# Output product and first up products of a decoder trunk: operands of y a block ahead, first combinations and up weights within the last block, a written order across the seam

## The chip, the cores and the metric

The kernel runs on one core of a Trainium2 chip. The metric is the device time of one execution in microseconds (us). The core has a matrix engine (TensorE, PE in the profile; the loading of its stationary operands is listed as PEld), a vector engine (VectorE, DVE), a scalar engine (ScalarE, ACT), a general engine (GpSimd, POOL) and SyncE (SP), which here issues all DMA transfers. Each engine works off its own queue in order; semaphores tie the queues together.

## The reference

A sequence of 2048 rows of width 1024, everything in float32. `mod` gives six vectors of the layer (shift, scale and gate of the mixer and of the FFN).

```python
h = rms_norm(x) * (1 + scale1) + shift1
p = h @ W_in                                  # all head groups in one projection
A, B, C = mlstm(p), forgetting_attention(p), gated_chunks(p)
x = x + gate1 * (concat(A, B, C) @ W_out)     # W_out 1024 x 1024
h = rms_norm(x) * (1 + scale2) + shift2
x = x + gate2 * ConvFFN(h)                    # up (d_ff 2816, twice), causal conv of width 3, SwiGLU, down
```

The change lies in the line with W_out, in the beginning of the up product, and in the last product of down.

## The kernel before, in words

The stages follow one another: projection, attention (until about 1124 us), the product with W_out, up, down. Each matrix operand is split into a rounded part (hi) and the remainder (lo), and `mm3` forms a product of two operands as three matmuls: hi by hi, hi by lo, lo by hi (lines L54, L55, L56). A split is a CAST on ACT (the hi) and a subtraction on DVE or POOL (the lo).

**The product with W_out.** The rows are done in four blocks of 512, in the order `TBS = (2, 3, 0, 1)`; so the second half of the sequence (H = 1) comes first. `Block.mm(i, nb)` makes 128 rows (i = 0..3) by 512 columns (nb = 0, 1) in one bank `wps`, from 8 k of y (`yhl`) and of W_out (`wo0` and `wo1`, its two halves of columns): 24 matmuls. One such (i, nb) is called a part. y is the mixer's output; it was stored to DRAM and is read back into the staging tiles `ld` (for the first four k from two places, which DVE adds), and then split. Before the change `Block.start` writes all 8 k at the head of the block that uses them, and the tiles come from two tags of 16 and 8 buffers.

`evict` multiplies a bank by the gate (`yg`), adds it to x and squares the result on ACT for the norm; `stats` turns the sums into a factor with a power on POOL (L128); `scale` multiplies the 1024 columns of x by it. When all four i of a block are scaled, `turns` transposes them: 8 k by 4 transposes of 128x128 into four banks `tps`, and for each k one ACTIVATE on ACT (L1240) that applies scale and shift and writes h (`hz`).

**Up.** The 22 groups of up weights for each half H are multiplied by a scheme with seven products p in place of eight, each on one combination of quarters of h: `OF = {1: "B11", 6: "T2", 2: "B21", 5: "T1", 7: "T3", 4: "T4", 3: "B22"}`. The B are quarters; T1, T3, T2 and T4 are differences. For the half that comes second (H = 1) the combinations are made during the output stage and stored (`put_d`, `hc_d`) and loaded again later; for the first half (H = 0) `b_first` makes them when it is needed: differences on DVE, CAST on ACT, lo on DVE (L1176 to L1185). A step is one product of one group: 12 matmuls into banks `ub`. The steps of the first two groups alternate: steps 0 and 1 use B11, 2 and 3 B21, 4 and 5 T1, 6 and 7 T2, 8 and 9 T3, 10 and 11 T4, 12 and 13 B22; step 14 is the first of the third group. `prep` makes the weights of a step three steps ahead: a sum or difference `S` of weight tiles `w` on DVE, then CAST (`wsph`, L1358) and lo (`wspl`, L1359) in 12 rotating buffers.

**Down** is made of seven products too, each of 11 steps k with four banks `db`; a step takes one k through all four banks. After the last step of the last product each bank goes through two operations on DVE (L1568, L1569) and out by DMA.

**What sets the order.** The program is written once in the order of the code; a scheduler then moves instructions within each engine's queue, and buffers (so many per tag) decide when a tile may be written again. Within `tc.manual_schedule()` it moves nothing, and each engine's queue follows the code. A pool is opened on the left or on the right side of the free memory and closed again, and a tile opened in a freed place waits for the last reader of what was there.

The matmuls of a step:

```python
def mm3(ps, lh, ll, rh, rl, start, stop, resume=False):
    T.matmul(ps, lh, rh, start=start, stop=False, skip_group_check=resume)
    T.matmul(ps, lh, rl, start=False, stop=False, skip_group_check=resume)
    T.matmul(ps, ll, rh, start=False, stop=stop, skip_group_check=resume)
```

## Time and profile before

| | |
|---|---|
| median of 3 runs | 2607.89 us (2607.47 to 2609.18) |
| the profiled execution | 2607.8 us, its span 2606.1 us |
| mean granted TensorE clock | 0.997 |
| output product, from the attention's last matmuls to its own last | 1124.57 to 1314.73 us |
| up, until its step 14 begins | 1314.73 to 1372.87 us |
| last matmul of down begins | 2599.58 us |

In a row of the timeline the columns are start (us), duration (us), engine, line, operation, output and inputs, shapes, count, and in square brackets the idle time of the engine before it with what ended it. A row "PE tps L1239 <- ACT hz L1240: 4.5, 3, 2.5" of the waits says that the matmuls of line 1239 into `tps` waited 4.5 us in total, three times, at most 2.5 us, for the operation of line 1240 on ACT.

### The profile page before, as it was taken

The page shows a single profiled execution, that of the slowest core. Times are in us where ns is not written, and L with a number is a line of the kernel's source. Part 1 is how long each engine was busy: PE and PEld are TensorE (multiplying, and loading weights), DVE is VectorE, ACT ScalarE, POOL GpSimd, SP SyncE. Part 2 cuts the span into 40 slices and gives each one's busy share as a digit, 9 for nine tenths or more (in the row PEclk, how much of TensorE's full clock was granted, in tenths as well). Part 3 has the DMA queues.
Part 4 walks back from the last instruction along what each step waited for, and adds up shares of the span by engine and source line. Part 5 has one row for each costly group of instructions (what it writes and reads, how often), then busy time and mean ns, then how long its engine had stood idle before and what let it go on. Part 6 is the DMA issues. An engine that isn't in the chain of part 4 may idle for free.

```text
span 2606.1 us, 36311 instructions
## 1 busy us (share of the span) xinstructions
PE 2530.5 (97%) x12521; PEld 2097.9 (81%) x12537; DVE 2010.0 (77%) x3438; ACT 1272.8 (49%) x2424; POOL 402.5 (15%) x532
## 2 busy tenths in 40 slices
PE   5999999999999999999989999999999999999999
PEld 5888888888787877777868888888888888888787
DVE  7657666476388889866589888888888887997797
ACT  4333343432388878844455544454444444444443
POOL 2012310132266556520000000000000000000000
PEclk9999999999999999999999999999999999999999
DMA  7345763454664445266632222255222217658523
GB/s 247 107 120 160 209 209 88 129 152 138 180 164 123 129 126 166 58 195 224 248 89 92 79 89 82 81 201 187 90 81 81 90 65 279 210 176 290 184 93 117
DMA packets 302592, 379.58 MB, mean 146 GB/s; under 512 B 31934, under 2 KB 194588, under 8 KB 300360
## 3 DMA queue, kind: packets, MB, share of 16 engines
q1 hardware_dynamic: 302408, 377.26, 46.1%
q8 instruction: 99, 1.62, 0.3%
q14 instruction: 85, 0.70, 0.1%
HBM read 276.44 MB, written 100.74 MB: 145 GB/s over the span
## 4 chain that ended last, share of the span: by engine, by line
PE 81%; DVE 9%; DMA 4%; ACT 3%; issue 2%; POOL 1%; SPq 0%; DVEq 0%; ACTq 0%; POOLq 0%
PE ub L56 11%; PE ub L54 11%; PE ub L55 11%; PE acc L54 6%; PE acc L56 6%; PE acc L55 6%; PE db L55 4%; PE db L56 4%; PE db L54 4%; PE sp L206 3%; PE tp L259 3%; PE op L245 2%; PE op L246 2%; PE wps L55 2%; PE wps L54 2%
## 5 line engine op out<-in xcount | busy, mean ns | idle before, releaser
L54 PE MATMUL acc<-wh,hh 128*128 128x512 f32 (+2 forms) x768 | 285.5, 373 | 1.9 <-DVE vhl L762 1.2
L54 PE MATMUL ub<-T,wsph 128*128 128x512 f32 x704 | 274.2, 390 | 5.8 <-ACT wsph L1358 5.8
L56 PE MATMUL ub<-T,wspl 128*128 128x512 f32 x704 | 273.7, 389 | 1.6 <-DVE wspl L1359 1.6
L56 PE MATMUL acc<-wh,hl 128*128 128x512 f32 (+2 forms) x768 | 274.2, 360 | 0.3 <-DVE hl L566 0.3
L55 PE MATMUL acc<-wl,hh 128*128 128x512 f32 (+2 forms) x768 | 273.9, 358 | 0.2
L55 PE MATMUL ub<-T,wsph 128*128 128x512 f32 x704 | 273.9, 389 | 0.0
L55 PE MATMUL db<-wspl,wsph 128*128 128x512 f32 x616 | 240.6, 391 | 3.6 <-DVE wspl L1490 3.5
L56 PE MATMUL db<-wsph,wspl 128*128 128x512 f32 x616 | 239.6, 389 | 0.0
L54 PE MATMUL db<-wsph 128*128 128x512 f32 x616 | 238.3, 389 | 0.3 <-ACT wsph L1489 0.3
L1358 ACT CAST wsph<-S 128x512 fp32r<-128x512 f32 x176 | 109.7, 623 | 228.4 <-PE ub L55 162.8
L263 DVE TENSOR_TENSOR plo<-tp,phi 128x512 fp32r<-128x512 f32 (+1 forms) x320 | 187.0, 607 | 31.6 <-ACT phi L262 29.4
L54 PE MATMUL ub<-B,wsph 128*128 128x512 f32 x528 | 207.1, 392 | 2.8 <-ACT wsph L1358 2.8
L56 PE MATMUL ub<-B,wspl 128*128 128x512 f32 x528 | 207.2, 392 | 0.6 <-DVE wspl L1359 0.6
L55 PE MATMUL ub<-B,wsph 128*128 128x512 f32 x528 | 207.0, 392 | 0.0
L223 ACT ACTIVATE L<-L,nm 128x1024 f32<-128x1024 f32 (+2 forms) x192 | 172.6, 903 | 36.0 <-DVE nm L212 34.7
L262 ACT CAST phi<-tp 128x512 fp32r<-128x512 f32 (+1 forms) x320 | 160.0, 521 | 40.2 <-PE tp L259 38.9
L259 PE MATMUL tp<-ident,L 128*128 128x128 f32 x1088 | 177.0, 274 | 2.5 <-POOL L L228 0.6
L206 PE MATMUL sp<-kk,q 128*128 128x512 f32 (+3 forms) x640 | 169.2, 375 | 3.3 <-DVE nm L212 2.2
L1489 ACT CAST wsph<-act 128x512 fp32r<-128x512 f32 x132 | 82.3, 623 | 179.0 <-PE db L55 162.2
L228 POOL TENSOR_SCALAR L<-L,rs 128x1024 f32<-128x1024 f32 (+2 forms) x192 | 167.2, 881 | 11.0
L56 PEld LDWEIGHTS acc<-wh,hl 128*128 128x128 f32 x768 | 145.0, 190 | 22.3 <-DVE hl L566 0.8
L54 PEld LDWEIGHTS acc<-wh,hh 128*128 128x128 f32 x768 | 146.2, 191 | 20.7 <-DVE vhl L762 1.4
(333 smaller groups left out, 5942.9 us busy)
## 6 DMA issues: line engine op xcount, KB each, us to landing
w<-in_w_up_dram SPq DMA_DIRECT2D x88, 512.0 KB
wd<-in_w_down_dram SPq DMA_DIRECT2D x176, 256.0 KB
wa<-in_w_ada_dram SPq DMA_DIRECT2D x96, 256.0 KB
act_d<-yc SPq DMA_DIRECT2D x44, 512.0 KB
act<-act_d SPq DMA_DIRECT2D x44, 512.0 KB
wr<-in_w_in_dram SPq DMA_DIRECT2D x64, 256.0 KB
q<-q_d SPq DMA_DIRECT2D x128, 128.0 KB
hc_d<-hl SPq DMA_DIRECT2D x28, 512.0 KB
```

Source lines behind the costliest of these rows:

```text
L54: T.matmul(ps, lh, rh, start=start, stop=False, skip_group_check=resume)
L55: T.matmul(ps, lh, rl, start=False, stop=False, skip_group_check=resume)
L56: T.matmul(ps, ll, rh, start=False, stop=stop, skip_group_check=resume)
L206: T.matmul(sp[:, b : b + bw], q2[n][:, qs], kk[:, s0 + b : s0 + b + bw], start=n == 0, stop=n == 1 and not last)
L223: A.activation(L[c], L[c], AF.Exp, bias=nm[:, n - 1 : n], scale=-1.0, accum_out=rs[:, c : c + 1])
L228: G.tensor_scalar(t, t, rs[:, 0:1], 1.0, op0=ALU.mult, op1=ALU.mult)
L245: T.matmul(op[:, c0:], vv[:, j, :], hi[:, c0:], start=(j == 0), stop=False)
L259: T.transpose(tp[:, i * P : (i + 1) * P], rows[i][j // 8][:, (j % 8) * P : (j % 8 + 1) * P], ident)
L262: A.copy(hi[:, c0:], tp[:, c0:])
L263: V.tensor_tensor(lo[:, c0:], tp[:, c0:], hi[:, c0:].bitcast(F32), op=ALU.subtract)
L1358: A.copy(hi, src)
L1489: A.copy(hi, v)
```

## The change

The parts of the change, in the order of the program:

- y is loaded and split one k at a time during the block before the one that uses it (`y_load`, `y_split`), into five staging tiles in place of three. Its tiles are the places `act4` to `act11` and `act14` to `act21`, which down uses later, one set for even blocks and one for odd.
- The second half of W_out is multiplied by the gate when it is loaded (`gain`), its lo are all made by DVE (before, every second one by POOL), and the eviction of the second half is one addition of bank and x.
- `turns` takes four k at a time: 16 transposes, a part of 24 matmuls, 16 transposes.
- The combinations that are stored for H = 1 are made a few operations at a time (`some`), and their four buffers are those of the up weights `w`.
- The last block runs by pairs of i (`by_two`). From its fifth part (n, j) = (3, 4) until step 14 of up the order is the written one. B11, B21 and the weights of the first up steps are made within the block's last parts, and the first step of up stands directly behind the block's last matmul.
- T1, T2, T3 and T4 and B22 of the first half lie in other tiles (`b_tile`), T1 and T3 are made with the next difference ahead of the present lo, and each is written at a fixed step.
- In down's last product the last three k are done bank by bank.
- The memset of `hal` goes from DVE to POOL, and pools that live across the seam (`keep_l`, `keep_r`) replace some that were closed there.

The core of the diff:

```diff
-        pool.open("wo_r", "right", ("yhl0", 2048, 16), ("ld", 2048, 3), ("wo0", 2048, 16))
-    def load_split(src, tag, eng, more=None):
+        pool.open("keep_r", "right", *[("act%d" % n, 4096, 1) for n in range(14, 22)])
+        pool.open("wo_r", "right", ("ld", 2048, 5), ("wo0", 2048, 16))
...
+        if gain is not None:
+            eng.tensor_tensor(t, t, gain, op=ALU.mult)
+        if pair:
+            both = pool.tile([P, 2, TB], F32R, name="yhl", tag=tag)
...
-    def load_w(nb):
+    def load_w(nb, gain=None):
         for k in range(KT):
             src = w_out[k * P : (k + 1) * P, nb * 512 : nb * 512 + 512]
-            wo.append(load_split(src, "wo%d" % nb, (G, V)[k % 2]))
+            eng = V if gain is not None else (G, V)[k % 2]
+            wo.append(split_parts(*load_parts(src), "wo%d" % nb, eng, gain=gain))
...
-        tag = {"T3": "act%d" % (14 + k), "T4": "act%d" % (18 + k)}.get(n, n)
+        at = {"T2": 0, "T1": 4, "T4": 8, "B11": 14, "B21": 18}
+        tag = "act%d" % (at[n] + k) if n in at else n
...
+    pool.open("keep_l", "left", *[("act%d" % n, 4096, 1) for n in range(4, 12)], ("w", 4096, 4))
     pool.open("zy", "left", ("zy", 4104, 8))
-    pool.open("wo_l", "left", ("hl", 4096, 4), ("gt1", 4096, 1), ("yg", 2048, 2), ("x2", 4096, 6), ("wst_", 8, 8))
-    pool.open("wo_r2", "right", ("ldx", 2048, 1), ("yhl1", 2048, 8), ("wo1", 2048, 16))
+    pool.open("wo_m", "left", ("wo1", 2048, 16))
+    pool.open("wo_l", "left", ("x2", 4096, 6), ("gt1", 4096, 1), ("yg", 2048, 2), ("wst_", 8, 8))
...
-    def load_y(n, tb):
-        tag = lambda k: "yhl%d" % ((n * 8 + k) % 12 >= 8)
-        part = lambda d, k: d[k * P : (k + 1) * P, tb * TB : (tb + 1) * TB]
-        return [load_split(part(yt_d, k), tag(k), V, part(y2_d, k) if k < 4 else None) for k in range(KT)]
+    ys, loaded_y = {}, []
+    def y_load(n, k):
+        part = lambda d: d[k * P : (k + 1) * P, TBS[n] * TB : (TBS[n] + 1) * TB]
+        loaded_y.append((n, k, load_parts(part(yt_d), part(y2_d) if k < 4 else None)))
+    def y_split():
+        while loaded_y:
+            n, k, parts = loaded_y.pop(0)
+            ys.setdefault(n, []).append(split_parts(*parts, "act%d" % ((4 if n % 2 else 14) + k), V, pair=True))
...
-        t = pool.tile([P, 2, 512], F32R, name="hl", tag="hl")
+        t = pool.tile([P, 2, 512], F32R, name="hl", tag="w")
...
+            if nb == 0:
+                V.tensor_tensor(t, self.ps.pop((i, nb)), gt1[:, ns], op=ALU.mult)
+                V.tensor_tensor(xt, xt, t, op=ALU.add)
+            else:
+                V.tensor_tensor(xt, self.ps.pop((i, nb)), xt, op=ALU.add)
...
+        def turns(self, ks):
+            for k in ks:
+                self.turn(k)
+            names = ("T1", "T3", "T2", "T4", "B22") if self.half else ("B11", "B21")
+            for group in (("T1",), ("B11",)) if ks[0] == 0 else (("T3",), ("T2", "T4", "B22"), ("B21",)):
+                for q in range(4):
+                    for n in group:
+                        if self.H == 1 and n in names:
+                            ops = {"T1": 2, "T3": 2, "T2": 3}.get(n, 1)
+                            todo.append((ops, lambda n=n, q=q: put_d(n, q)))
...
+        def difference(q):
+            if minus and q < 4:
+                V.tensor_tensor(h_part(n, q), h_part("B12" if n == "T1" else "B22", q), h_part(minus, q), op=ALU.subtract)
+                A.copy(hb[0, n][q][:, 0, :], h_part(n, q))
+        if minus:
+            difference(0)
+        for q in qs:
+            t = hb[0, n][q]
+            if minus:
+                difference(q + 1)
+                V.tensor_tensor(t[:, 1, :], h_part(n, q), t[:, 0, :].bitcast(F32), op=ALU.subtract)
...
+            if more and self.H == 1 and k > KH - 4:
+                ks = range(KH - 3, KH) if k == KH - 1 else ()
+            got = [self.sl.pop((p, j)) for j in ks]
             for i in range(4):
                 sl = slice(i * P, (i + 1) * P)
-                mm3(self.ps[p][i], ah[:, sl], al[:, sl], bh, bl, not more and k == 0, k == KH - 1, resume=more)
+                for j, (ah, al, bh, bl) in zip(ks, got):
+                    mm3(self.ps[p][i], ah[:, sl], al[:, sl], bh, bl, not more and j == 0, j == KH - 1, resume=more)
...
+    by_two = [(i + m, nb) for m in (0, 2) for nb in range(2) for i in range(2)]
+    prev = before = None
+    for k in range(KT):
+        y_load(0, k)
+        y_split()
+    written = ExitStack()
+    for n, tb in enumerate(TBS):
+        blk = Block(n, tb)
+        for j, (i, nb) in enumerate((by_nb, by_i, by_i, by_two)[n]):
+            if (n, j) == (3, 4):
+                written.enter_context(tc.manual_schedule())
+            if (n, j) == (0, 4):
+                load_w(1, gt1[:, 512:1024])
+            blk.mm(i, nb)
+            if (n, j) == (3, 3):
+                w_first = [w_load(0), w_load(1)]
+            if prev:
+                prev[0].evict(*prev[1:])
+            y_split()
+            if prev and prev[2] == 1:
+                prev[0].stats(prev[1])
+            some({1: 2, 2: 5, 3: 3}.get(n, 0))
+            if (n, j) == (3, 7):
+                prep(2)
+            if prev and prev[2] == 1:
+                prev[0].scale(prev[1], pool.tile([P, D], F32, name="x2") if (n, j) == (3, 7) else None)
+            if (n, j) == (3, 5):
+                pool.close("wo_r")
+                up_open_right()
+                for _ in range(AHEAD):
+                    up_groups(-1)
+            if (n, j) == (3, 6):
+                prep(0)
+                prep(1)
+            if (n, j) == (3, 7):
+                prep(4)
+            if before and j in ((2, 3) if n == 3 else (1, 2)):
+                assert n < 3 or not todo
+                before.turns(range(4) if j == (2 if n == 3 else 1) else range(4, 8))
+            if n == 3 and 4 <= j <= 6:
+                if j == 4:
+                    b_first("B11")
+                else:
+                    b_first("B21", (2 * j - 10, 2 * j - 9))
+            if n < 3:
+                for k in {5: (5, 6), 6: (7,), 7: ()}.get(j, (j,)):
+                    y_load(n + 1, k)
+            prev = (blk, i, nb)
+        before = blk
...
+    assert not todo and not loaded_y
     blk.evict(3, 1)
-    b_first("B21", (0, 1))
+    prep(3)
     blk.stats(3)
-    b_first("B21", (2,))
-    blk.scale(3, True)
-    b_first("B21", (3,))
-    prep(2)
+    blk.scale(3, pool.tile([P, D], F32, name="x2"))
+    pp.close("wo_r")
+    pp.open("up_r", "right", ("ub0", 2048, 4))
+    mm_up = lambda i: groups[steps[i][1], steps[i][2]].mm(steps[i][3])
+    mm_up(0)
+    groups[0, 0].post(1)
+    prep(5)
+    blk.turns(range(4))
+    mm_up(1)
+    b_first("T1")
+    groups[0, 1].post(1)
+    blk.turns(range(4, 8))
+    pp.close("wo_l")
+    pp.open("up_l", "left", ("ub1", 2048, 4))
+    pool.close("wo_l")
+    pool.close("wo_m")
+    up_open_left()
+    hal = pool.tile([P, 44, 2], F32, name="hal")
+    G.memset(hal, 0.0)
+    mm_up(2)
+    mm_up(3)
+    late.append(steps[2])
+    pool.open("up_r2", "right", *[("act%d" % n, 4096, 1) for n in range(4)])
+    prep(6)
+    b_first("T2")
...
+        if i + AHEAD in (9, 11, 13):
+            b_first({9: "T3", 11: "T4", 13: "B22"}[i + AHEAD])
+        if i == 14:
+            written.close()
```

TensorE behind the first block's last part: `wps` is the output product, `tps` a transpose, and the number behind x is one block row of 128. Before, the rows are:

```order
L56 MATMUL wps<-wo1h,yhl0l 128x512
L1239 MATMUL tps<-ident,x_13194 128x128
L1239 MATMUL tps<-ident,x_13222 128x128
L1239 MATMUL tps<-ident,x_13254 128x128
L1239 MATMUL tps<-ident,x_13286 128x128
...
L54 MATMUL wps<-wo0h,yhl1h 128x512
...
L55 MATMUL wps<-wo0l,yhl1h 128x512
...
L56 MATMUL wps<-wo0h,yhl1l 128x512
```

After, the same place reads:

```order
L56 MATMUL wps<-wo1h,yhl 128x512
L1259 MATMUL tps<-ident,x_13205 128x128
L1259 MATMUL tps<-ident,x_13237 128x128
L1259 MATMUL tps<-ident,x_13277 128x128
L1259 MATMUL tps<-ident,x_13317 128x128
...
L54 MATMUL wps<-wo0h,yhl 128x512
L55 MATMUL wps<-wo0l,yhl 128x512
L56 MATMUL wps<-wo0h,yhl 128x512
...
L1259 MATMUL tps<-ident,x_13205 128x128
...
L54 MATMUL wps<-wo1h,yhl 128x512
```

Before, all 32 transposes stand together, with single matmuls of the next part among the last of them; after, two groups of 16 have the 24 matmuls of a part between them.

TensorE at the end of the last block and the beginning of up (`ub`; B_ with a number is a tile of a combination). Before:

```order
L56 MATMUL wps<-wo1h,yhl0l 128x512
L1239 MATMUL tps<-ident,x_14437 128x128
L1239 MATMUL tps<-ident,x_14474 128x128
L1239 MATMUL tps<-ident,x_14811 128x128
...
L54 MATMUL ub<-B_14766,wsph 128x512
L55 MATMUL ub<-B_14766,wsph 128x512
L56 MATMUL ub<-B_14766,wspl 128x512
...
L1239 MATMUL tps<-ident,x_14830 128x128 x4
L1239 MATMUL tps<-ident,x_14437 128x128
...
L54 MATMUL ub<-T_14934,wsph 128x512
```

After:

```order
L56 MATMUL wps<-wo1h,yhl 128x512
L54 MATMUL ub<-B_14653,wsph 128x512
L55 MATMUL ub<-B_14653,wsph 128x512
L56 MATMUL ub<-B_14653,wspl 128x512
...
L56 MATMUL ub<-B_14656,wspl 128x512
L1259 MATMUL tps<-ident,x_14413 128x128
L1259 MATMUL tps<-ident,x_14457 128x128
L1259 MATMUL tps<-ident,x_14789 128x128
L1259 MATMUL tps<-ident,x_14810 128x128
...
L54 MATMUL ub<-B_14653,wsph 128x512
```

Before, 12 transposes of the first three block rows follow the last output matmul, and the rest come after steps 0 and 1; after, step 0 follows it, then 16 transposes, and step 1.

DVE at the same seam, from the eviction of the last bank on (line numbers of each program: L1185, L1294 and L1204 make a lo of a combination, L1359 and L1339 one of a weight, L1231 and L1251 are the scale). Before:

```order
L1217 TENSOR_TENSOR yg<-wps,gt_13132 128x512
L1185 TENSOR_TENSOR B_14766<-hz,B_14766 128x512
L1185 TENSOR_TENSOR B_14769<-hz,B_14769 128x512
...
L1218 TENSOR_TENSOR x_14594<-x_14594,yg 128x512
L1185 TENSOR_TENSOR B_14818<-hz,B_14818 128x512
...
L1359 TENSOR_TENSOR wspl<-w_14753,wsph 128x512
L1225 TENSOR_TENSOR st<-st 128x1
...
L1226 TENSOR_SCALAR st<-st 128x1
...
L1231 TENSOR_SCALAR x_14830<-x_14594,st 128x1024
...
L1181 TENSOR_TENSOR hz<-hz 128x512
```

After:

```order
L1238 TENSOR_TENSOR x_14665<-wps,x_14665 128x512
L1339 TENSOR_TENSOR wspl<-w_14575,wsph 128x512
L1245 TENSOR_TENSOR st<-st 128x1
L1246 TENSOR_SCALAR st<-st 128x1
L1251 TENSOR_SCALAR x_14810<-x_14665,st 128x1024
L1328 TENSOR_TENSOR S_14832<-w_14576 128x512
L1329 TENSOR_TENSOR S_14833<-S_14832,w_14575 128x512
L1339 TENSOR_TENSOR wspl<-S_14832,wsph 128x512
L1285 TENSOR_TENSOR hz<-hz 128x512 x2
L1294 TENSOR_TENSOR T_14877<-hz,T_14877 128x512
```

Before, eight lo of B11 and B21 stand between the last eviction and the last scale; after, one lo of a weight does, and the operations of B11 and B21 stand in the parts ahead of it.

More of the change, by code (lines that the diff above doesn't have):

```diff
@@ L1342, in prep @@
             A_ = self.A
-            n = OF[p]
-            if (self.H, self.g) == (0, 0) and (0, n) not in hb:
-                b_first(n)
             if p in (5, 6) and self.S1 is None:
```

135 lines of the change are left out of this document (38 added, 97 removed).

## The prediction

> **What bounds the kernel now.** I read the page first, then the waits of TensorE (PE), then the windows of the stages, then the order of time at the seams.
>
> ```profile
> span 2606.1 us, 36311 instructions
> PE 2530.5 (97%) x12521; PEld 2097.9 (81%) x12537; DVE 2010.0 (77%) x3438; ACT 1272.8 (49%) x2424; POOL 402.5 (15%) x532
> PE ub L54 <- ACT wsph L1358: 7.4, 2, 4.6
> PE tps L1239 <- ACT hz L1240: 4.5, 3, 2.5
> ```
>
> PE is busy 97% of the span, so only the remainder and half-speed stretches can be won. The last two rows (PE's waits from 1113 to 1373 us) say where: at the output stage's transposes, and where up begins. The profiled execution took 2607.8 us (span 2606.1 and 1.7 around it), 0.1 below the median of 2607.89; the sum is made against 2607.8.
>
> Windows (us, then busy time of PE, PEld, DVE, ACT, POOL, then granted clock, DMA share, GB/s):
>
> ```profile
> 1124.57:1314.73 190.16, 186.12 (x856) 152.89 (x856) 110.53 (x191) 73.26 (x148) 14.39 (x19) 0.99 0.66 226
> 1314.73:1372.87 58.14, 47.98 (x202) 37.78 (x201) 52.53 (x88) 37.47 (x71) 0.84 (x1) 0.91 0.27 77
> 1329.44:1424.40 94.96, 88.72 (x388) 72.46 (x389) 94.14 (x137) 57.03 (x102) 0.00 (x0) 0.98 0.24 77
> 1424.40:2220.00 795.60, 794.41 (x3505) 657.34 (x3504) 660.87 (x875) 380.71 (x624) 0.00 (x0) 1.00 0.35 118
> 1230.68:1234.09 3.41, 3.02 (x12) 2.65 (x13) 3.31 (x6) 3.41 (x6) 0.00 (x0) 0.50 0.76 213
> 1319.43:1326.25 6.82, 6.22 (x16) 4.50 (x15) 4.90 (x10) 2.22 (x6) 0.84 (x1) 0.50 0.44 134
> 1336.49:1339.90 3.41, 3.18 (x7) 2.44 (x8) 3.41 (x7) 3.41 (x8) 0.00 (x0) 0.50 0.00 0
> ```
>
> The first row is the output product after the attention, the second the seam to up (until step 14 of up), the third what DVE has to do there, the fourth steady up, where PE is full at full clock and nothing can be won. The last three show a granted clock of 0.50, each behind an idle PE:
>
> ```profile
> 1177.71 1.91 PE L1239 MATMUL tps<-ident,x 128*128 128x128 f32 x16
> 1181.04 0.66 PE L1239 MATMUL tps<-ident,x 128*128 128x128 f32 x4 [1.42 <-ACT hz L1240]
> 1231.07 1.11 PE L1239 MATMUL tps<-ident,x 128*128 128x128 f32 x4 [2.52 <-ACT hz L1240]
> 1314.73 1.47 PE L1239 MATMUL tps<-ident,x 128*128 128x128 f32 x12
> 1319.01 0.50 PE L54 MATMUL ub<-B,wsph 128*128 128x512 f32 x1 [2.81 <-ACT wsph L1358]
> 1320.50 0.80 PE L56 MATMUL ub<-B,wspl 128*128 128x512 f32 x1 [0.60 <-DVE wspl L1359]
> 1329.46 2.66 PE L1239 MATMUL tps<-ident,x 128*128 128x128 f32 x16 [0.54 <-ACT hz L1240]
> 1336.72 0.80 PE L54 MATMUL ub<-T,wsph 128*128 128x512 f32 x1 [4.60 <-ACT wsph L1358]
> 1372.64 0.39 PE L56 MATMUL ub<-B,wspl 128*128 128x512 f32 x1
> 1372.87 0.39 PE L54 MATMUL ub<-B,wsph 128*128 128x512 f32 x1
> ```
>
> The last two start 0.227 apart: that is a matmul's price in a dense stream, so a step of 12 costs 2.72. Sixteen transposes cost about 1.85 when nothing holds them.
>
> **1. Output stage.** The window holds 856 PE records, 96 of them transposes: 760 × 0.227 = 172.5, and six sixteens at 1.85 = 11.1, together 183.6. It took 190.2, so 6.6 us are lost: the waits of 1.42 and 2.52 for transpose banks, the half clock behind the second (1.7), switches of shape where transposes and products alternate singly, and a late y load. The change writes each set of 32 transposes as two sixteens with 24 products (5.4 us) between. One sixteen fills four banks; ACT empties a bank in 0.68 (5.46/8, row below), four in 2.7: less than 5.4, so the banks are free, and the waits go with their half clock. The y loads and splits stand a block earlier, in idle time of DVE (110.5 of 190.2 busy). I charge 1.4 back, two operations of 0.69: y parts of the second block now stand in DVE's order before the attention's last splits, and one of them waits for a load. Net gain 5; bounds 2 (only the two waits' 3.9 go, less 1.4, rounded down) and 8 (all 6.6, and the 1.4 the other way).
>
> The gate on the second half of the weights adds 8 DVE multiplications and brings 4 subtractions from POOL; 16 others leave DVE with the shorter eviction. What counts is how late each weight is: the first is needed some 20 us after 1124.57 (the 88 products or so left of the first half), the eighth some 5 us later.
>
> ```profile
> 1131.90 0.69 DVE L1217 TENSOR_TENSOR yg<-wps,gt 128x512 f32<-128x512 f32 x1 [4.10 <-DMA gt<-gt_d]
> 1141.47 0.80 SPq L297 DMA_DIRECT2D ld<-in_w_out_dram  x2
> 1144.25 1.22 ACT L131 CAST wo1h<-ld 128x512 fp32r<-128x512 f32 x2 [2.10 <-DMA ld<-in_w_out_dram]
> ```
>
> The gate is there by 1131.9. A load takes 2.8 (1141.47 to 1144.25), the gate 0.60, cast 0.61, remainder 0.69: 4.7 in sequence, while five buffers let up to five overlap; even two at a time need 8 × 4.7 / 2 = 19 from 1131.9, about 1151, which is when PE wants the eighth. Cost 0, bounds 0 and 5.
>
> The 28 stores of combinations for the other half use the four buffers of the first up weights now. The four loads of these weights stand on SP's queue in the fourth part of the last block, so they wait for the last stores; four parts of 24 products (22 us) follow before step 0, and a load of this stage took 2.8. Cost 0, bounds 0 and 3.
>
> **2. Seam to up.** Let E be the end of the last output product (1314.73). Before, step 14 begins at E + 58.1. Without waits that is 14 × 2.72 + 2 × 1.85 = 41.8; 16 us are lost to the waits above and to three half-clock units of 3.41. Now up's first product follows at once, and the last row block's chain runs beside it:
>
> ```profile
> 1315.54 2.49 DVE L1185 TENSOR_TENSOR B<-hz,B 128x512 fp32r<-128x512 f32 x4
> 1311.03 0.63 ACT L1219 ACTIVATE yg<-x 128x512 f32<-128x512 f32 x1 [4.75 <-DVE x L1218]
> 1314.70 3.74 ACT L1184 CAST B<-hz 128x512 fp32r<-128x512 f32 x7 [2.95 <-PE wps L55]
> L128 POOL TENSOR_TENSOR st<-st,nhalf 128x1 f32<-128x1 f32 x16 | 9.6, 603 | 166.3 <-DVE st L1226 166.3
> 1312.89 0.75 DVE L1231 TENSOR_SCALAR x<-x,st 128x1024 f32<-128x1024 f32 x1 [0.75 <-POOL st L128]
> 1328.63 5.46 ACT L1240 ACTIVATE hz<-tps,sh,a 128x512 f32<-128x512 f32 x8 [6.98 <-PE tps L1239]
> 1329.44 0.69 DVE L1181 TENSOR_TENSOR hz<-hz 128x512 f32<-128x512 f32 x1 [4.67 <-ACT hz L1240]
> 1370.95 0.68 DVE L1359 TENSOR_TENSOR wspl<-S,wsph 128x512 fp32r<-128x512 f32 x1
> ```
>
> Eviction 0.69 with its hand-over: E + 0.9. Square and its read-out to 1.7, a cast in ACT's order (0.53) to 2.3, DVE's remainder of a weight (0.60) and two small operations to 3.25, POOL's power 0.60, the scale 0.75: E + 4.8. Step 0 ends at 2.7, so PE idles 2.1. Then sixteen, step 1, sixteen: 11.2. Steps 2 to 7 end at 27.5 if T1 and T2 come in time: T2 has one scratch tile, so each of its four parts is difference, cast, remainder in sequence, 2.3; from the second four evictions, with T1's casts between them, at about 14.4 it ends at 23.6, in time. T3 is behind that on DVE, 13 operations of 0.60 (2.49/4) and a hand-over: remainders 29.8 to 32.7. Step 8, which would end at 30.2, ends at 33.2: a wait of 3. B22's remainders come at 44.9, 18 operations and hand-overs on; step 12 loses 1.4, and step 14 begins at E + 48.1. That is 10.0 sooner.
>
> It is not all kept. From 1329.44 DVE works without a gap (94.14 of 94.96 in its window). Its own lead with the change: B22's last remainder at 44.9 against 46.5 before (1.6), six operations of 0.60 more done by then (3.7), together 5.3. Before, a weight's remainder ends at 1371.6 (last row above); step 15 begins at 1372.87 + 2.72 and reads it two products later, 1376.0: 4.4 in hand. PE can keep 5.3 + 4.4 = 9.7 of the 10.0. I take 9; bounds 5 (only DVE's lead, rounded down) and 11 (the wait for T3 shorter).
>
> The tiles of the weight combinations lie elsewhere and are the first loads of down; each is last read before its load is needed, so 0, bounds -1 and 1. The memset that goes to POOL is 0: POOL has 0.84 us of work in that window.
>
> **3. The end.**
>
> ```profile
> 2599.58 0.39 PE L56 MATMUL db<-wsph,wspl 128*128 128x512 f32 x1
> 2597.97 1.37 DVE L1568 TENSOR_TENSOR o<-db,gt 128x512 f32<-128x512 f32 x2 [4.39 <-PE db L56]
> 2601.66 1.28 DVE L1569 TENSOR_TENSOR o<-o,s 128x512 f32<-128x512 f32 x2
> 2592.89 0.69 DVE L1490 TENSOR_TENSOR wspl<-wd,wsph 128x512 fp32r<-128x512 f32 x1
> ```
>
> DVE's eight operations for four banks begin at 2597.97 and run to 2602.94, three us past PE, because the banks finish within 2 us of each other. Bank by bank they finish 2 us apart, so only the last bank's two operations stand behind PE: end at 2601.3, 1.64 sooner. Against it: the last k is needed three products into the first bank, while its remainder ends at 2593.58 and its tiles come free only with the fourth last k: a wait of 0.4. Net 1.2, bounds 0 and 1.7.
>
> **Sum.** 5 + 9 + 1.2 = 15.2: 2607.8 - 15.2 = 2592.6, and by the median 2592.7.
>
> **A rule against it.** PE now idles 2.1 and then runs sixteen transposes (1.85): 4.0 us without a product. Before, 1.42 + 1.91 = 3.3 without a product left no stretch at 0.50, while 2.52 + 1.91 = 4.4, and the 4.3 from 1314.73 to 1319.01, each did; 4.0 lies between. A unit at half clock costs 3.41 / 2 = 1.7, and part of that DVE's shortage would hide. The Trainium skill, "TensorE: Matmul & The Clock Gate", Part 1, says that the clock halves after an idle window of about 3.4 us that runs freely, and Part 4 that transposes don't count as busy in the same way. The trace agrees on the length (3.41 and 6.82) and shows nothing against the second; whether 4.0 us hold a window then hangs on its phase, which no row tells.
>
> **Rivals.** (a) DVE gives back all but its lead: the seam brings 5.3, the total is 11.5, 2596.3. For it: 94.14 of 94.96; against: the 4.4 in hand. (b) A unit at half clock behind the first transposes, as above: 1.7 less, 2594.4. For it the 4.3 and 4.4, against it the 3.3. (c) The other side: the gated half weights come one at a time, because buffers also wait for y parts in the same five. Then 8 × 4.7 = 38 from 1131.9 instead of 19; PE waits some 19, and the kernel ends near 2612. It decides once PE waits over 15 us there. Against: each needs its buffer only until its remainder, and the queue row above shows two issued together. (d) The change doesn't do what it says: transposes still wait, y still comes late; only the seam's first waits (2.81, 0.60) go and the end's 1.2: 2603, within 0.2%.
>
> **How the numbers follow.** 0.2% (5.2 us) is about what a measurement of this kernel can tell from no change. Chances: my sum 0.38, (b) 0.29, (a) 0.20, (d) 0.06, (c) 0.07. The first three all lie below 2602.7: faster 0.87, same 0.06, slower 0.07. The range takes the bounds of the three terms: 2607.8 less 8, 11 and 1.7 is 2587, less 2, 5 and 0 is 2601. (c) and (d), 0.13 together, stay outside.
>
> **What would show it.** PE's waits "tps <- ACT hz" gone between 1124 and 1310, and the stage 5 us shorter; up's first product directly behind the last output product, then about 2 us idle ahead of the transposes and one wait of about 3 for T3; granted clock 1.0, or one stretch at 0.50 there; DVE without a gap until step 14 or later; DVE's last operation 1.7 us behind the last matmul. I am wrong if PE waits for gated weights near 1150, if new waits for remainders follow step 14, or if the attention ends later.

## The result, and the profile after

The median after is 2618.37 us (2615.57 to 2621.39, 7 runs), before 2609.24 us (7 runs). The ratio is 1.0034, with an interval of 1.0022 to 1.0045: slower by a third of a per cent, where 2592.7 us, 0.6% faster, was predicted. The profiled execution of after took 2621.4 us, the longest of its seven, and is set against the 2607.8 us of before.

```profile
span 2619.7 us, 36326 instructions
PE 2545.7 (97%) x12537; PEld 2100.0 (80%) x12537; DVE 2007.9 (77%) x3433; ACT 1269.7 (48%) x2424; POOL 398.6 (15%) x529
```

These are the span and the first row of the page. PE has 15.2 us more busy time than before (2530.5), though the change adds no matmul (before, 16 records of matmuls are missing; the weight loads are 12537 in both). Read from the timelines, from the start of the last matmul of one stage to that of the next (the seam to the start of step 14):

| stage (us) | before | after | predicted change | measured |
|---|---|---|---|---|
| projection, up to its last matmul | 710.27 | 712.37 | 0 | +2.1 |
| attention | 414.19 | 416.18 | +1.4, in the 5 below | +2.0 |
| output product | 190.04 | 186.03 | -5 with the row above | -4.0 |
| seam, to step 14 | 58.36 | 57.78 | -10.0 | -0.6 |
| up, from step 14 | 806.55 | 820.92 | +1 | +14.4 |
| down | 420.17 | 421.49 | 0 | +1.3 |
| from the last matmul to the end | 8.22 | 6.63 | -1.2 with the row above | -1.6 |

Over all kernels of this study the projection, which none of them changes, ends between 709.3 and 713.2 us, and down takes 418.5 to 423.0; +2.1 and +1.3 lie inside that. Much of the first row and part of the second is granted clock. In the profiled execution of after, three units of 3.41 us at half clock lie ahead of the output product, two in the projection and one in the attention; before has none there:

```profile
215.15:218.56 3.41, 3.41 (x10) 2.63 (x9) 2.77 (x8) 0.00 (x0) 1.75 (x2) 0.50 0.03 13
546.24:549.65 3.41, 3.24 (x12) 2.98 (x13) 2.84 (x8) 0.00 (x0) 0.90 (x1) 0.50 0.30 106
1119.68:1123.09 3.41, 3.41 (x15) 2.94 (x15) 0.67 (x2) 1.07 (x2) 1.34 (x2) 0.50 0.77 211
```

The executions with two such units behind 200 us took 711.6 to 713.2 us for the projection, the others 709.3 to 711.0. Two rows need a cause: up and the seam.

The windows of output product, seam, two stretches of the seam and steady up, after (columns as in the prediction):

```profile
1128.60:1314.80 186.20, 186.13 (x860) 153.13 (x859) 111.12 (x197) 79.11 (x158) 10.01 (x15) 1.00 0.69 235
1314.80:1372.37 57.57, 46.91 (x202) 38.28 (x201) 45.18 (x71) 29.18 (x54) 0.72 (x2) 0.88 0.26 83
1321.05:1324.46 3.41, 3.22 (x14) 3.17 (x15) 3.38 (x6) 2.64 (x5) 0.00 (x0) 0.50 0.00 0
1348.37:1358.61 10.24, 5.72 (x14) 4.49 (x15) 9.41 (x16) 6.22 (x14) 0.00 (x0) 0.50 0.39 108
1450.00:2100.00 650.00, 648.81 (x2813) 527.52 (x2812) 534.69 (x702) 305.22 (x502) 0.00 (x0) 1.00 0.31 104
```

The output product now is PE's without a gap, at full clock. In the seam PE is busy for 46.9 of 57.6 us, four units of 3.41 us at half clock included. The last row is the surprise: PE full, full clock, and only 2813 matmuls in 650 us, one in 231 ns. Before, the same window holds 2862, one in 227 ns:

```profile
1450.00:2100.00 650.00, 648.81 (x2862) 536.80 (x2861) 544.33 (x716) 310.13 (x510) 0.00 (x0) 1.00 0.32 106
```

PE's waits from 1113 to 1440 us, and its timeline at the seam (matmuls within steps left out):

```profile
PE ub L54 <- ACT T L1203: 7.4, 1, 7.4
PE tps L1259 <- DVE x L1251: 3.2, 1, 3.2
```

```profile
1314.81 0.39 PE L54 MATMUL ub<-B,wsph 128*128 128x512 f32 x1
...
1317.54 0.49 PE L1259 MATMUL tps<-ident,x 128*128 128x128 f32 x3
1321.24 3.03 PE L1259 MATMUL tps<-ident,x 128*128 128x128 f32 x13 [3.22 <-DVE x L1251]
1323.93 0.73 PE L54 MATMUL ub<-B,wsph 128*128 128x512 f32 x1
...
1327.01 1.91 PE L1259 MATMUL tps<-ident,x 128*128 128x128 f32 x16
...
1352.89 0.76 PE L54 MATMUL ub<-T,wsph 128*128 128x512 f32 x1 [7.44 <-ACT T L1203]
```

Up's first product follows at once, and the waits "tps <- ACT hz" are gone, both as predicted. But the first idle time is 3.2 in place of 2.1, with the sixteen at half clock behind it, and step 8 begins 38.1 us after E (1314.81). What DVE does in that time:

```profile
1316.69 0.68 DVE L1238 TENSOR_TENSOR x<-wps,x 128x512 f32<-128x512 f32 x1
1318.73 0.69 DVE L1339 TENSOR_TENSOR wspl<-w,wsph 128x512 fp32r<-128x512 f32 x1 [1.36 <-ACT wsph L1338]
...
1320.43 0.76 DVE L1251 TENSOR_SCALAR x<-x,st 128x1024 f32<-128x1024 f32 x1 [0.75 <-POOL st L128]
...
1325.66 0.69 DVE L1294 TENSOR_TENSOR T<-hz,T 128x512 fp32r<-128x512 f32 x1 [1.16 <-ACT T L1286]
...
1332.53 0.69 DVE L1339 TENSOR_TENSOR wspl<-S,wsph 128x512 fp32r<-128x512 f32 x1 [2.99 <-ACT wsph L1338]
...
1340.98 0.69 DVE L1204 TENSOR_TENSOR T<-t,T 128x512 fp32r<-128x512 f32 x1
...
1343.62 0.69 DVE L1339 TENSOR_TENSOR wspl<-S,wsph 128x512 fp32r<-128x512 f32 x1 [0.74 <-ACT wsph L1338]
1344.23 0.68 DVE L1331 TENSOR_TENSOR S<-w,w 128x512 f32<-128x512 f32 x1
1345.68 0.69 DVE L1339 TENSOR_TENSOR wspl<-S,wsph 128x512 fp32r<-128x512 f32 x1 [0.76 <-ACT wsph L1338]
...
1350.07 1.46 DVE L1294 TENSOR_TENSOR T<-hz,T 128x512 fp32r<-128x512 f32 x2
1351.45 0.68 DVE L1339 TENSOR_TENSOR wspl<-w,wsph 128x512 fp32r<-128x512 f32 x1
1352.06 0.68 DVE L1368 TENSOR_TENSOR u<-ub,s 128x512 f32<-128x512 f32 x1
```

DVE stands idle for 7.8 us in these six waits. Four, 5.9 us together, are for a CAST of a weight: written order has each remainder (L1339) as DVE's next operation, and DVE does nothing that stands behind it meanwhile. The longest, 2.99, is for a cast that itself stands on ACT behind four evictions of transposes. The waits row names a cast of line 1203 as what step 8 waited for. At that time these are the casts of T4, which step 8 doesn't read; T3's own (L1286) end at 1350.8. But step 8 also reuses the bank of step 6, and that is emptied by the eviction `u` (L1368), which stands in DVE's order behind all of T3 and one more weight; step 8 begins 0.15 us after it (1352.06 + 0.68 = 1352.74).

At the end (PE's last matmul, then DVE):

```profile
2614.76 0.39 PE L56 MATMUL db<-wsph,wspl 128*128 128x512 f32 x1
```

```profile
2615.19 0.69 DVE L1552 TENSOR_TENSOR o<-db,gt 128x512 f32<-128x512 f32 x1 [0.62 <-PE db L56]
2615.91 0.69 DVE L1553 TENSOR_TENSOR o<-o,s 128x512 f32<-128x512 f32 x1
```

Only one bank's two operations stand behind PE, as the prediction had it.

### The profile page after: what moved, and what is told of

Read it like the earlier page. It is cut to its first block, busy times and chain, and to the rows that moved or that the text cites. A ratio compares the mean times of both kernels' runs of the same rounds, so it can differ in the third digit from the quotient of the medians.

```text
span 2619.7 us, 36326 instructions
## 1 busy us (share of the span) xinstructions
PE 2545.7 (97%) x12537; PEld 2100.0 (80%) x12537; DVE 2007.9 (77%) x3433; ACT 1269.7 (48%) x2424; POOL 398.6 (15%) x529
## 5 line engine op out<-in xcount | busy, mean ns | idle before, releaser
L54 PE MATMUL ub<-T,wsph 128*128 128x512 f32 x704 | 278.3, 396 | 8.6 <-ACT T L1203 7.4
L55 PE MATMUL ub<-T,wsph 128*128 128x512 f32 x704 | 278.0, 395 | 0.0
L54 PEld LDWEIGHTS ub<-T,wsph 128*128 128x128 f32 x704 | 132.8, 189 | 40.5 <-ACT T L1203 7.8
```

## Experiments: why steady up is slower

Seven steps, one of each product, make a group: 19.040 us before and 19.373 us after, to 1 ns in every group but those at the seam and at the change to the second half. Up has 44 groups: 14.7 us. The steps differ. Before, each takes 2.720 us; after, B21 still does, T1, T3, T4 and B22 take 2.79 to 2.80, and B11 and T2 2.735. PE's timeline of after, at T1, T3 and T4 in a row:

```profile
1613.32 0.40 PE L54 MATMUL ub<-T,wsph 128*128 128x512 f32 x1
...
1621.72 0.39 PE L54 MATMUL ub<-B,wsph 128*128 128x512 f32 x1
```

36 matmuls take 8.40 us, 233.3 ns each, with no wait on any; the B21 step ahead of them runs at 226.7. B11 and T2 lose only on the first three matmuls behind a longer step, 5 ns each.

What sets these steps apart is where their operands lie. The built program gives each tile's address, in bytes within a partition; here modulo 256:

```
                      before   after
weights wsph, wspl      224      96
B11, B21, T2            224      96
T1, T3, T4, B22         224     224
```

The change keeps a small pool of the attention (`att_s`) open on the right side until the end of the kernel, where before it was closed ahead of up. Its twelve tiles of 8 bytes stand 32 bytes apart, so it takes 384 bytes, which is 128 modulo 256. So all that lies on the right moved to 96; what lies on the left stayed at 224. T1 and B22 lay on the left before, and the change puts T3 and T4 there too. The output product shows the same: before both operands lie at 96; after, each block has one half of W_out at the address of its y and one half at the other, and the second runs at 233 ns. Four halves of 96 matmuls at 6.4 ns more are 2.5 us.

**Theory A: a matmul is slower when the addresses of its two operands differ modulo 256.** The rival: the pool structure or the neighbours of the new tiles (stores, writes of other engines) do it. Two kernels test it from both sides: 128 bytes more on the right in after make the addresses equal again; the same in before make them unequal, with nothing else changed.

```diff
-        pool.open("keep_r", "right", *[("act%d" % n, 4096, 1) for n in range(14, 22)])
+        pool.open("keep_r", "right", *[("act%d" % n, 4096, 1) for n in range(14, 22)], ("pad", 128, 1))
```

> The changed kernel with 128 bytes more at the foot of the right-hand stack, so that every tile on the right moves by 128 bytes and nothing else changes. Theory A (a matmul whose two operands lie at addresses that differ by 128 modulo 256 takes 233.3 ns in place of 226.7): all pairs agree now, so up runs at 226.7 ns, a group of seven steps in 19.04 us in place of 19.37, the output product too; 14.7 + 2.4 = 17 us less than the changed kernel, about 2601, ratio to the kernel before about 0.997. Rival B (what counts is that one operand lies in the left and one in the right part of the memory, or how far apart): no change, 19.37 us per group, ratio 1.003. Rival C (the slower matmuls come from other traffic at that time): no change.

In before (second kernel):

```diff
-        pool.open("up_r1", "right", *[("act%d" % n, 4096, 1) for n in range(14, 22)], ("wsp", 2048, 12))
+        pool.open("up_r1", "right", *[("act%d" % n, 4096, 1) for n in range(14, 22)], ("wsp", 2048, 12), ("pad", 128, 1))
```

> The kernel before with 128 bytes at the foot of the right-hand stack from up on. Theory A: the pairs of T1 and of B22 (left) with the weights (right) disagree now, the other five agree: two steps in seven at 233.3 ns, 19.04 + 0.17 = 19.21 us per group, 44 groups, 7.5 us slower, ratio 1.003. Rivals B and C: no change, ratio 1.000.

Windows of steady up, first of after with the pad, then of before with it:

```profile
1450.00:2100.00 650.00, 648.81 (x2862) 536.74 (x2861) 543.68 (x716) 310.16 (x508) 0.00 (x0) 1.00 0.32 106
```

```profile
1450.00:2100.00 650.00, 648.81 (x2836) 531.89 (x2835) 539.33 (x710) 306.46 (x505) 0.00 (x0) 1.00 0.31 105
```

The pad gives after its matmuls back (2862, a group again 19.040): median 2601.28 us (11 runs), ratio 0.998 (0.9971 to 0.9988). It takes them from before (2836, a group 19.213): 2614.26 us (6 runs), ratio 1.003 (1.0018 to 1.0042). There T1 and B22, the two left at 224, take 2.79; the steps moved along with the weights don't. 128 bytes that nobody reads or writes decide; the rival is out. In the padded after, T1 and T4 differ from the weights by 256 modulo 512, T3 and B22 by 0, and all run at 226.7: equal modulo 256 is enough.

Which operands, and by how much must they differ? One kernel has the pad between two pools on the right, so that weights and T2 return to 224 but B11 and B21 stay at 96; two others have 64 and 96 bytes, which leave differences of 64 and 32.

```diff
+        pool.open("pad_r", "right", ("pad", 128, 1))
...
-    for n in ("dn_l", "keep_l", "dn_r", "up_r2", "up_r1", "keep_r", "att_s"):
+    for n in ("dn_l", "keep_l", "dn_r", "up_r2", "up_r1", "pad_r", "keep_r", "att_s"):
```

> The changed kernel with the 128 bytes between the tiles of B11 and B21 (they stay) and the rest of the right-hand stack (moves). Theory A: B11 and B21 become the slow steps, T1, T3, T4, B22 and T2 run at 226.7 ns: 19.04 + 0.19 = 19.23 us per group; in the output product the blocks with y on the right are slow with both halves of the weights and those with y on the left fast: 6 us less than the changed kernel in all. Rival B: T1, T3, T4 and B22 stay slow, 19.37 us.

```diff
-        pool.open("keep_r", "right", *[("act%d" % n, 4096, 1) for n in range(14, 22)])
+        pool.open("keep_r", "right", *[("act%d" % n, 4096, 1) for n in range(14, 22)], ("pad", 64, 1))
```

> The changed kernel with 64 bytes in place of 128, so that left and right differ by 64 modulo 128. Theory A says nothing of 64. If the penalty belongs to a unit of 256 bytes, some of it shows: 233 ns or a value between 226.7 and 233 for T1, T3, T4 and B22; if only a difference of exactly 128 costs, 19.04 us per group. Rivals B and C: 19.37.

```diff
-        pool.open("keep_r", "right", *[("act%d" % n, 4096, 1) for n in range(14, 22)])
+        pool.open("keep_r", "right", *[("act%d" % n, 4096, 1) for n in range(14, 22)], ("pad", 96, 1))
```

> The changed kernel with 96 bytes in place of 128: left and right differ by 32 modulo 256. If any difference within 256 bytes costs: T1, T3, T4 and B22 at some 233 ns, 19.4 us per group. If only multiples of 64 do: 19.04.

| kernel | difference modulo 256 | steps at 233.3 ns | a group (us) | time (us) |
|---|---|---|---|---|
| before | 0 | none | 19.040 | 2607.8 |
| after with 128 | 0 | none | 19.040 | 2602.4 |
| before with 128 | 128 | T1, B22 | 19.213 | 2611.8 |
| after, 128 between the pools | 128 | B11, B21 | 19.213 | 2612.6 |
| after | 128 | T1, T3, T4, B22 | 19.373 | 2621.4 |
| after with 64 | 64 | T1, T3, T4, B22 | 19.40 | 2617.6 |
| after with 96 | 32 | T1, T3, T4, B22 | 19.413 | 2620.2 |

(Times are of the profiled executions.) Which steps are slower follows the pairs of addresses every time; 32 is already too much, and nothing under 32 was tried. One pair falls out: with 64, the output product's pair of y on the left and W_out on the right took about 229 ns in six of its eight parts and 233.3 only in two.

## Experiments: why the seam gained nothing

All these have the 128 bytes, so the first of them stand against the first experiment's seam of 57.11 us and its 2601.28 us. Where steps 13 to 16 wait or mix with one another, the start of step 14 says too little, so the start of step 21 is given; with the pad alone it is 76.61 us after the last output product.

**Theory B: DVE's written order makes PE late at the seam; single entries can be moved. The rival: the whole order limits, and what is moved waits elsewhere.** First, T3, T4 and B22 are written behind the evictions that free banks:

```diff
-        prep(i + AHEAD)
-        if i + AHEAD in (9, 11, 13):
-            b_first({9: "T3", 11: "T4", 13: "B22"}[i + AHEAD])
+        if i not in (7, 8):
+            prep(i + AHEAD)
...
+        if i in (7, 8, 10):
+            b_first({7: "T3", 8: "T4", 10: "B22"}[i])
+        if i in (7, 8):
+            prep(i + AHEAD)
```

> On top of the 128-byte pad: T3, T4 and B22 are written behind the evictions u of the banks (line 1368) and not ahead of them, and the weights of steps 10 and 11 behind T3 and T4. Theory A2: step 8 waits for 7.6 us because the eviction of its bank stands on DVE behind the whole of T3. With the eviction ahead, step 8 follows the first part of T3, about 4 us sooner, and the wait falls to some 3.5 us; step 14 begins 3 to 5 us sooner than with the pad alone (54 in place of 57.1 us after the last output product), and the kernel takes some 2597. Rival: DVE's own work is the limit (it has 45 us to do there), so what is won at step 8 comes back as waits at steps 10 to 14, and step 14 is at most 1 us sooner.

```profile
PE tps L1259 <- DVE x L1251: 3.4, 1, 3.4
PE ub L54 <- ACT wsph L1338: 2.3, 2, 1.6
PE ub L54 <- ACT T L1286: 1.7, 1, 1.7
PE ub L55 <- DVE T L1294: 0.7, 3, 0.2
PE ub L54 <- DVE u L1368: 0.5, 1, 0.5
```

2605.33 us (one time). The wait at step 8 falls from 7.6 to 1.7, and new ones come in its place (PE's waits, above): step 21 begins at 78.01, 1.4 later than with the pad alone. The rival is right.

Second, step 1 stands ahead of the first sixteen transposes, and step 2 between the sixteens:

```diff
-    blk.turns(range(4))
     mm_up(1)
+    blk.turns(range(4))
+    mm_up(2)
...
-    mm_up(2)
```

> On top of the 128-byte pad: step 1 of up stands ahead of the first sixteen transposes and step 2 between the two sixteens, so PE has 5.4 us of products while the last row block is evicted and scaled. Theory A3: the first idle time (3.0 us) almost goes, and with it the half clock of the transposes (16 in 1.7 us in place of about 3); the chain on DVE starts 1.4 us sooner, but PE comes to step 8 some 4.7 us sooner, so the wait there grows from 7.6 to about 11 us, and step 14 is 1.4 us sooner. Rival: PE's idle time itself is what is lost, and step 14 is 4 us sooner.

2600.87 us, seam 57.14. The first wait falls from 3.0 to 0.6, a wait of 2.0 appears at a product of up, and the 7.6 at step 8 stay: no gain. The kernel with 64 bytes shows the same from another side. It idles 3.0 us ahead of the transposes too, but no half clock follows; its step 1 begins 1.3 us sooner than with 128 bytes (7.86 against 9.15 after the last output product), and its step 8 at the same 38.09. So the half clock behind the first transposes is not what makes step 8 late.

Third, for the output stage, the y loads of its second block three parts later:

```diff
-                for k in {5: (5, 6), 6: (7,), 7: ()}.get(j, (j,)):
+                for k in ({3: (0, 1), 4: (2, 3), 5: (4, 5), 6: (6, 7)}.get(j, ()) if n == 0 else {5: (5, 6), 6: (7,), 7: ()}.get(j, (j,))):
```

> On top of the 128-byte pad: the loads of the second block's y start three parts later, so none of them stands in DVE's order among the attention's last splits. Theory A4: those loads delay the end of the attention by 1.3 us (from the end of the projection to the last product of the attention 415.6 us, before the change 414.2), so it comes back to 414.3, and the rest stays. Rival: the 1.3 us come from elsewhere: no change, or PE waits for y at the second block.

2597.94 us: attention 415.06 (0.6 less), output 183.33 (0.8 less), seam 56.39. The 1.3 does not come back: over all kernels of this study with the later loads the attention took 414.98 to 415.58 us, over those with the change's loads 415.16 to 416.18, a few tenths apart. So the rival is right for most of it, and why the attention ends about 1 us later is open.

All three together:

> The 128-byte pad and the last three edits together. By the theories the seam is 5 to 7 us shorter than with the pad alone and the attention 1.3: about 2594, ratio to the kernel before 0.995. By the rival of a full DVE the seam gives 1 to 2: about 2598, 0.997.

2603.74 us (11 runs), ratio 0.9986 (0.9977 to 0.9995); step 21 begins at 76.40, where the later loads alone had 76.01. They don't add.

**Theory C: not what the order says but that it is written.** Four kernels, on top of the pad and the later y loads: the written order ends at step 4; there is none; it stays, but each weight remainder is deferred behind DVE's next operation, so that a cast no longer holds the queue; and the last with the first two moves added.

```diff
-        if i == 14:
+        if i == 4:
             written.close()
```

> On top of the pad and the later y loads: the written order ends at step 4 of up and not at step 14, so the scheduler orders DVE from T2 on. Theory A5: in the seam DVE is not full (with the pad 41 of 50 us busy from 1320 to 1370); the written order makes it wait for ACT between each weight's sum, cast and remainder, and puts the eviction of a bank behind the whole of T3. In the scheduler's order T3 and T4 lie among T2's operations and the sums come early: step 14 begins 3 to 6 us sooner, 51 to 54 us after the last output product in place of 56.4. Rival: half clock and the late start of the chain are what is lost; no more than 1 us.

```diff
-            if (n, j) == (3, 4):
-                written.enter_context(tc.manual_schedule())
```

> The same without any written order: the scheduler sets the last half block and the seam too. Theory A5: the part until step 4 gains nothing by being written except that step 0 follows the last output product at once; step 14 within 1 us of the run with the written order until step 4. Rival: without the written order the first steps of up wait for B11 and weights as before the change, 58 us.

```diff
...
-            V.tensor_tensor(lo, src, hi.bitcast(F32), op=ALU.subtract)
+            pend.append(lambda: V.tensor_tensor(lo, src, hi.bitcast(F32), op=ALU.subtract))
+            if not in_written[0]:
+                flush()
...
```

> The written order kept, but each weight's remainder on DVE is written one operation later, behind the next sum or difference, so DVE does not wait for the cast between. Theory A5: about six waits of 0.74 and the 1.4 ahead of the last scale go, 4 to 5 us sooner at step 14 (51.5 to 52.5). Rival: the waits for the cast only move to T2's chain; no more than 1 us.

> The deferred remainders with T3 and T4 behind the evictions and step 1 ahead of the transposes. Theory A5 and A2 together: 49 to 51 us to step 14, the kernel about 2592. Rival of a limit on DVE: no better than the deferral alone.

| kernel | seam (us) | start of step 21 (us) | time (us, one each) |
|---|---|---|---|
| pad alone | 57.11 | 76.61 | 2602.4 |
| pad and later y loads | 56.39 | 76.01 | 2597.9 |
| these, written to step 4 | 51.25 | 70.29 | 2596.0 |
| these, no written order | 42.40 | 61.44 | 2588.6 |
| these, remainders deferred | 51.30 | 70.43 | 2594.6 |
| these, deferred, and steps moved | 48.50 | 70.97 | 2595.0 |

Deferring the remainders alone brings 5.1 us (56.39 to 51.30): waiting for casts in the written order is one part of it. What is left there is 1.4 us ahead of the first transposes and one wait of 4.9 us of step 8, now named as the eviction (DVE u): the second part, order by step. With the steps moved as well, step 14 comes sooner but step 21 does not (70.97 against 70.43). Written to step 4, the wait of step 8 falls to 1.1 and 3.4 ahead of the first transposes stay; so by these single runs 5.1 of the 14.0 us that come without a written order belong to the order behind step 4, and 8.9 to the order ahead of it. Without a written order the seam takes 42.40, where 14 steps and two sixteens without a wait are 41.8. Both forecasts for it, some 58 and the same as "written to step 4", were wrong. The kernel without written order again, with more runs, and the change as it is, less the written order alone:

> The pad, the later y loads and no written order, timed in rounds. By the look at it (step 14 begins 42.4 us after the last output product, 0.6 above the sum of the products and transposes, and up keeps its 19.04 us per group): 2587 to 2592, ratio to the kernel before 0.993.

> The change as it is, with the written order taken out and nothing else: no pad, y loads as in the change. If the two causes add, it keeps the 17 us of the slow operand pairs and wins the 14 us of the seam: about 2604, ratio 0.998; 19.37 us per group, step 14 some 43 us after the last output product. If the gain of the scheduler's order needs the pad or the later loads: above 2612.

With the pad: 2587.43 us (4 runs), ratio 0.9917 (0.9903 to 0.993), so faster than both kernels. Without it: 2605.02 us (11 runs), ratio 0.9985 (0.9976 to 0.9994), seam 42.90, a group 19.373. Neither cause hides the other: the written order costs about 14.9 us of seam with unequal addresses as well (57.78 less 42.90).

Windows, PE's and DVE's timelines of the kernel with the pad and no written order:

```profile
1128.15:1311.87 183.72, 183.72 (x861) 153.28 (x860) 116.52 (x206) 81.22 (x161) 10.33 (x15) 1.00 0.70 238
1311.87:1354.08 42.21, 42.10 (x201) 34.75 (x200) 39.57 (x65) 29.04 (x57) 0.72 (x2) 1.00 0.36 113
1316.11:1410.00 93.89, 93.78 (x424) 77.55 (x423) 92.57 (x134) 56.98 (x104) 0.17 (x1) 1.00 0.32 101
1450.00:2100.00 650.00, 648.81 (x2862) 536.69 (x2861) 544.58 (x717) 310.14 (x508) 0.00 (x0) 1.00 0.32 106
```

```profile
1311.64 0.39 PE L56 MATMUL wps<-wo1h,yhl 128*128 128x512 f32 x1
1311.87 1.03 PE L1259 MATMUL tps<-ident,x 128*128 128x128 f32 x8
1312.66 0.48 PE L54 MATMUL ub<-B,wsph 128*128 128x512 f32 x1
```

```profile
1319.89 2.49 DVE L1294 TENSOR_TENSOR T<-hz,T 128x512 fp32r<-128x512 f32 x4
1322.52 0.69 DVE L1195 TENSOR_TENSOR t<-hz 128x512 f32<-128x512 f32 x1
1323.13 0.69 DVE L1285 TENSOR_TENSOR hz<-hz 128x512 f32<-128x512 f32 x1
...
1335.17 1.29 DVE L1294 TENSOR_TENSOR T<-hz,T 128x512 fp32r<-128x512 f32 x2
1336.37 0.69 DVE L1339 TENSOR_TENSOR wspl<-w,wsph 128x512 fp32r<-128x512 f32 x1
1336.98 0.68 DVE L1368 TENSOR_TENSOR u<-ub,s 128x512 f32<-128x512 f32 x1
```

The scheduler puts the eight transposes of rows already scaled right behind the last output product, where the written order has step 0; and between T2's operations on DVE (L1195) it puts T3's differences (L1285) and weights. T3 ends 24.6 us after E (1336.46 less 1311.87), where in after it ends 36.7 after. DVE is as full as before the change, 92.57 of 93.89 us, and PE has 93.78 of 93.89 beside it.

## Why the prediction was wrong

By the profiled executions 2621.4 less 2592.6 are 28.8 us missed. 15.8 are addresses (up 820.92 less 806.97 with the pad, output 186.03 less 184.17), 8.8 the seam (9 kept against 0.2: -0.6 there, and +0.4 in up with the pad), 2.1 the projection with its two units at half clock, and 2.0 the rest of attention, output, down and end. From the medians, each against its own before, the pad is worth 14.5 us (+9.1 and -5.4), and taking out the written order together with the later y loads another 15.8 (-5.4 and -21.2).

- **"The tiles of the weight combinations lie elsewhere ... so 0, bounds -1 and 1."** This step failed, and by most. A tile's place was costed only by when it is loaded and last read. Place also set the rate of the products that read it: 17 us by the groups (14.7, two of the 44 groups in the seam) and halves (2.5, of which 1.9 show in the stage's time). The same blind spot stands in "steady up, where PE is full at full clock and nothing can be won": nothing could be won, but something lost, and PE still reads full at 1.00. The Trainium skill, "SBUF — State Buffer", section "Operand start alignment", says that an operand must start at a multiple of its element size and that this is "about legality, not speed". All addresses here obey it, and 6.6 ns a matmul were lost all the same.
- **Seam, "10.0 sooner", of which 9.** Failed in its size: 0.6. By its own walk PE loses 2.1 + 3 + 1.4; it lost 5.1 up to step 7, 7.4 at step 8 and 3.2 behind it, where the half clock lasts until 1358.6. The walk took DVE's operations one behind the other and left out most of DVE's waiting in a written queue (7.8 us in six waits, 5.9 of them for casts of weights), and it priced step 8 by T3's remainders alone, not by the eviction behind them.
- **"DVE works without a gap", so PE can keep 9.7 at most.** Wrong too, on the other side: without written order the seam is 15.9 us shorter (58.36 less 42.44) and up is 806.57 against 806.55. Nothing is given back. A DVE that was busy throughout did not hold PE up: what counted was in which order it did the work. So the mechanism of rival (a) is wrong too.
- **Output stage 5 sooner.** Right with the addresses equal: 190.04 to 184.17, less 1.4 in the attention, 4.4. In after 2.0. The waits for `hz` went with their half clock, and the attention ended 1.4 later with the pad and 2.0 in after. That agrees with the charge of 1.4 for y parts only by luck: with these loads moved away, most of it stayed. A smaller reading was off too: sixteen transposes, taken at 1.85 us, hold PE for 1.66 until the next product starts (1327.01 to 1328.67 in after).
- **Gated weights 0.** Right, and rival (c) wrong: with the pad PE waits for them 0.2 us twice. The kernel became slower, but not by the mechanism of the rival that was to cover that side.
- **End 1.2.** 1.6 behind the last matmul. The 0.4 charged against it can't be told from down's spread.
- **Rival (b)** happened, and more than it: one unit at half clock behind the first transposes and three around step 8. The kernel with 64 bytes had about the same idle time and no unit behind the transposes, as the prediction said that it would hang on the phase; and the unit there cost nothing at step 8. The Trainium skill, "TensorE: Matmul & The Clock Gate", Part 1, says that the window of 3.4 us runs freely; the trace agrees, as the half clock sets in at 1321.06 and at 1348.37, 27.31 apart, eight times 3.41.
- **Rival (d)** wrong: the change does what it says; transposes no longer wait for banks.

What stays open: why operands at unequal addresses cost 6.6 ns a matmul, why one pair at 64 cost less, why the attention ends later, and which operations ahead of step 4 make the written order lose 8.9 us there.

## What to carry to other kernels

When a change opens, closes or keeps a pool, compare the addresses of both operands of the hot matmuls before and after, and count matmuls in a fixed window: neither busy share nor clock shows a slower stream. Measure an order written by hand against the scheduler's own: here each operation of the written queue that waited for another engine held all that stood behind it. Where a wait names one releaser, look also for the last reader of the bank that is to be reused.

## What was not expected of the hardware

A dense stream of 128x512 fp32r matmuls ran at 226.7 ns each where stationary and moving operand had the same address modulo 256, and at 233.3 ns where they differed by 32, 64 or 128, at full granted clock and with no wait shown (one pair at 64 excepted, 229 ns). The first three to five matmuls behind such a stretch cost 15 to 24 ns more in all. Other shapes, types and differences under 32 were not measured.
